# Strassen's scheme for the input product of two FFNs in a float32 transformer forward pass

## The chip, the cores and the metric

The kernel runs on one core of a Trainium2 chip. A core has five engines that run side by side, each with its own queue of instructions: TensorE (PE in the profile; its weight loads are listed apart as PEld), VectorE (DVE), ScalarE (ACT), GpSimd (POOL) and SyncE (SP), which here issues the transfers from the chip's memory (HBM) to the on-chip memory (SBUF). TensorE writes its sums to PSUM, from which VectorE and ScalarE read. The metric is the device time of one execution in microseconds. Three runs of the kernel before gave 1662.89, 1662.97 and 1663.38 us: median 1662.97.

## The reference

Two layers work on 256 latent tokens (LAT) and 256 context tokens (CTX) of width 1024, all in float32. Layer 0 is half FFN, attention, half FFN; layer 1 is half FFN, mLSTM, half FFN, and the last one is computed for the latent tokens alone. So there are four half FFNs; the change is in the second (layer 0, after attention) and the third (layer 1, before mLSTM):

```python
def half_ffn(h, shift, scale, gate, w_in, w_out, g, b):
    xm = modulate(h, shift, scale)               # h * (1 + scale) + shift
    a, u = jnp.split(xm @ w_in, 2, axis=-1)      # w_in: 1024 x 5632
    y = (jax.nn.silu(a) * u) @ w_out             # w_out: 2816 x 1024
    return post_norm(h, 0.5 * gate * y, g, b)    # LayerNorm(ALPHA * h + ...)
```

`shift`, `scale` and `gate` are slices of `silu(c) @ ada_w + ada_b`, nine per layer and one set for each of the two conditioning vectors (latent, context). Since they don't depend on the tokens, the kernel computes them ahead, in pieces, on VectorE: these pieces are the "dots" below.

## The kernel before

Activations lie transposed: 128 partitions carry 128 of the 1024 features, `xh[:, k, :]` holds block k (0 to 7) for 512 columns, of which 0 to 255 are LAT and 256 to 511 are CTX. Every float32 operand x of a large product is split into a rounded part h and the remainder l = x - h (`split`: a cast on ScalarE, then a subtraction on VectorE), and each 128 x 128 block of a product is three matmuls, `mm3`: wh by xh, wh by xl, wl by xh (lines 227, 230, 231 of the profile). Weights come in chunks of 128 x 1024 floats, 512 KB each, over SP's queue into one of three `raw` buffers (RAW = 3), and their split goes to one of seven `w` buffers (WB = 7).

The hidden width 2816 is 22 blocks of 128, called units. `ffn` works in two halves (`hf` = 0, 1) of 11 units. In each half come first the input products: unit j multiplies its block of the columns of `w_in`, for both parts (a and u), with all eight blocks of x, into two PSUM banks; `ffn_g` makes silu(a) * u and splits it. Then come the output products: for each of the eight output blocks d, `unit_out` adds up 11 blocks of `w_out` with the 11 stored units, and VectorE adds the result, times the gate, to h. Units 0 to 3 of a FFN (LEAD = 4) are done for LAT and CTX apart, 256 columns at a time, since the LayerNorm of the FFN or mixer before them ends for LAT first. So are the last four output blocks (TAIL = 4) of the second half. All other input and output products have 512 columns.

A unit takes two chunks of `w_in`, eight blocks each. Before, the blocks of a chunk alternate between a and u: block `k * 2 + part`.

Dots: `ada` loads one chunk of `ada_w` (`ada_load`, two `ada` buffers, the same queue of SP) and multiplies it with the silu of a conditioning row kept in `cb`, 1024 columns, with a running sum (`ada_dot`), once or twice, for one or two conditioning vectors. `side(...)` hands `ffn` a function that is called after each unit and after each output block of the first half, and that issues the next two items of a queue. `queue[1]` (40 items of two vectors, used in the second FFN) and `queue[2]` (32 items of one vector, used in the third) are the ones that the change touches.

The order within an engine's queue is made by a scheduler from the order of the program, priorities and its own estimates of durations; an engine executes its queue strictly in that order, so an instruction that waits holds up those behind it. Buffers of a pool with n copies are reused as they come free, and the wait for that is put in by the framework. PSUM has six `mm` banks for these products and two others.

Of the kernel before, what the change touches and what calls it, by code (L numbers as in the profile page):

```python
# [9 lines left out]
F32 = mybir.dt.float32  # L10
F32R = mybir.dt.float32r
# [3 lines left out]
ALU = mybir.AluOpType  # L15
# [107 lines left out]
C_MASK = 128  # L123
C_ROPE = C_MASK + 2 * TL
C_N = C_ROPE + 4 * P


class Stream:
# [29 lines left out]
class Body:  # L158
# [65 lines left out]
    def mm3(self, out, w, x, first, last, pin=False):  # L224
        (wh, wl), (xh, xl) = w, x
        mm = self.nc.tensor.matmul
        ins = mm(out, wh, xh, start=first, stop=False)  # L227
        if pin:
            self.pin(ins)
        mm(out, wh, xl, start=False, stop=False)  # L230
        mm(out, wl, xh, start=False, stop=last)  # L231

    def x(self, d, g):
        return self.xh[:, d, g[0] : g[1]], self.xl[:, d, g[0] : g[1]]
# [38 lines left out]
    def silu_c(self):  # L273

        pool = ExitStack()
        self.n += 1
        p = pool.enter_context(self.tc.tile_pool(name=f"cp{self.n}", bufs=1, side="right"))
        self.cb = self.t([P, 2, D], pool=p)
        return pool

# [27 lines left out]
    def ada_load(self, layer, dt):  # L308
        if (layer, dt // ND) not in self.mod:
            self.mod[layer, dt // ND] = self.t([P, 2, ND])  # L310
        r = self.t([P, 1024], tag="ada", bufs=2, pool=self.gp)
        self.nc.sync.dma_start(r, self.a["ada_w"][layer, dt])
        return r

# [235 lines left out]
            V.tensor_tensor(out=sl, in0=sl, in1=pu[:, :n], op=ALU.mult)  # L550
        self.split(sl, gh[:, t0:t1], gl[:, t0:t1])

    def ffn(self, layer, s, gate, groups, side, start=None):
        nc, V = self.nc, self.nc.vector
        li = layer * 2 + s
        allg = BOTH
        call = lambda *k: side.get(k, lambda: None)()
        with self.tc.tile_pool(name=f"ffn{li}", bufs=1) as gp:
            self.gp, self.gt, self.gw, self.gn = gp, {}, T, NFH
            done = 0  # L560
            if start:
                start(self)
                done = NSTART

            def unit_in(j, w, g, steps={}, ks=range(ND), ps=None):
                n = g[1] - g[0]
                pa, pu = ps or (self.mm(), self.mm())
                for k in ks:
                    for part, o in ((0, pa), (1, pu)):
                        self.mm3(o[:, :n], w(k * 2 + part), self.x(k, g), k == 0, k == ND - 1)  # L570
                    self.steps(steps.get((j, k), ""))
                if ks[-1] < ND - 1:
                    return pa, pu
                self.ffn_g(j, pa, pu, g)

            def unit_out(hf, d, w, g, steps={}):
                t0, t1 = g
                y = self.mm()
                for i in range(NFH):
                    gh, gl = self.gt[hf * NFH + i]  # L580
                    self.mm3(y[:, : t1 - t0], w(d * NFH + i), (gh[:, t0:t1], gl[:, t0:t1]), i == 0, i == NFH - 1)
                    self.steps(steps.get((int(g == CTX), d - (ND - TAIL), i), ""))
                for gg in groups:
                    if gg[0] >= t0 and gg[1] <= t1:
                        v = 0 if gg[0] == 0 else 1
                        z = self.h[:, d, gg[0] : gg[1]]
                        V.scalar_tensor_tensor(z, y[:, gg[0] - t0 : gg[1] - t0], gate()[:, v, d : d + 1], z, ALU.mult, ALU.add)  # L587
                        if hf:
                            self.add_sum(gg, d)

            w_in, w_out = self.a["ffn_in"][li], self.a["ffn_out"][li]
            stream = lambda j: Stream(self, [w_in[2 * j + i] for i in range(2)])
            for hf in range(2):
                js = list(range(hf * NFH, (hf + 1) * NFH))[0 if hf else done :]
                if hf == 0 and not start:
                    first = js[:LEAD]
                    ws = {j: Keep(self, [w_in[2 * j + i] for i in range(2)], SH) for j in first}
                    assert len(self.running) == 1

                    k0, k1 = range(ND // 2), range(ND // 2, ND)  # L600
                    for j in first[:-1]:
                        unit_in(j, ws[j], LAT, LEADSTEP[li])
                    j = first[-1]
                    ps = unit_in(j, ws[j], LAT, ks=k0)
                    assert not self.running
                    pc = unit_in(first[0], ws[first[0]], CTX, ks=k0)
# [7 lines left out]
                    js = js[LEAD:]  # L614
                for j in js:
# [9 lines left out]
                body = ND - TAIL if hf else ND  # L625
                for d in range(body):
                    unit_out(hf, d, w, allg)
                    call("out", hf, d)
                if body < ND:
                    w = Keep(self, w.chunks, SH, w)  # L630
                    self.fine = True
                    for g in groups:
                        for d in range(body, ND):
                            unit_out(hf, d, w, g, TAILSTEP)
                    self.steps('B')


    def ffn_last(self, layer, gate):
# [3 lines left out]
        with self.tc.tile_pool(name="ffnl", bufs=1) as gp:  # L642
# [9 lines left out]
            def unit_in(j, g, steps={}):  # L652
                n = g[1] - g[0]
                w, pa, pu = stream(j), self.mm(), self.mm()
                for k in range(ND):
                    for part, o in ((0, pa), (1, pu)):
                        self.mm3(o[:, :n], w(k * 2 + part), self.x(k, g), k == 0, k == ND - 1)
                    self.steps(steps.get((j, k), ""))
                return pa, pu

# [798 lines left out]
def emit(ctx, tc, a, out):  # L1459
# [5 lines left out]
    both2 = (0, 1)  # L1465
    queue = [
        [(0, p, both2) for p in range(16, 72)],
        [(1, p, both2) for p in range(40)],
        [(1, p, (0,)) for p in range(40, 72)],
    ]  # L1470
    made = {}

    def once(key, f):
        def get():
            if key not in made:
                made[key] = f()
            return made[key]
        return get

    def side(key, coef, keep=(True, True), nxt=True, ada=(), alone=False):  # L1480
        def pop():
            for _ in range(3 if len(ada) > 40 else 2):
                if ada:
                    b.ada(*ada.pop(0))

        get = once(key, coef)

        b.begin = lambda g: b.norm(g, get, keep[0 if g == LAT else 1], nxt, alone)
        s = {}
        for j in range(NF):  # L1490
            s["in", j] = pop
        for d in range(ND):
            s["out", 0, d] = pop
        return s

    both = (LAT, CTX)
# [4 lines left out]
    cpool = b.silu_c()  # L1501
    b.silu_load()
    b.silu()
    b.ffn(0, 1, once("g1", lambda: b.half_gate(0, 8)), both, side("n2", lambda: b.ln_mod(0, 2, (1, 0)), ada=queue[1]))
    assert not queue[1]
    b.ffn(1, 0, once("g2", lambda: b.half_gate(1, 2)), both, side("n3", lambda: b.ln_mod(1, 0, (1, 3)), (True, False), ada=queue[2]))
    assert not queue[2]
    cpool.close()
# [7 lines left out]
def _layout(inputs):  # L1516
# [13 lines left out]
    w_in = w.reshape(4, NF, P, 2, 1024).transpose(0, 1, 3, 2, 4).reshape(4, 2 * NF, P, 1024).copy()  # L1530
    A["ffn_in"] = w_in
# [73 lines left out]
```

## Time and profile before

| what | value |
|---|---|
| median of the runs | 1662.97 us |
| profiled execution: span | 1662.0 us (1.0 below the median of the runs; instructions from first to last) |
| TensorE busy | 1639.8 us, 99% |
| TensorE weight loads | 1439.4 us, 87% |
| VectorE busy | 1209.0 us, 73% |
| ScalarE busy | 670.5 us, 40% |
| second FFN, units of 512 columns begin | 610.78 us |
| third FFN, units of 512 columns begin | 978.38 us |

A group's row gives the line in the kernel, the engine, the operation, what it writes and reads (all tiles are called t), the shape, the count, then total busy time, the mean in ns, and the idle time of the engine before such an instruction with what ended it. A row of the timeline gives start, length, engine, line, operation, and in brackets the idle time ahead of it and what ended that. Matmuls are pipelined: one's printed length reaches into the next, so what one costs is the distance from start to start.

### The profile page before, as it was taken

To read this page: it belongs to the slowest core of one execution; us is meant where nothing else is said; L and a number is where in the kernel's file an instruction comes from. 1 tells how busy PE (TensorE), PEld (TensorE's weight loads), DVE (VectorE), ACT (ScalarE), POOL (GpSimd) and SP (SyncE) were. 2 spreads that over 40 slices of the span, in tenths; PEclk is the share of its full clock that TensorE was granted. 3 is DMA by queue.
4 is the path that set the end of the run, shared out by engine and by line. 5 is a ranking of instruction groups with operands and counts; after the bars stand their busy time and mean duration, and the time that the engine had idled before them with its cause. 6 is when DMAs were issued, how large, how long until landed. Compare 5 with 4: busy or idle time off the path is not lost. (4 is left out here: it accounts for less than half of the span.)

```text
span 1662.0 us, 24616 instructions
## 1 busy us (share of the span) xinstructions
PE 1639.8 (99%) x9516; PEld 1439.4 (87%) x9516; DVE 1209.0 (73%) x2465; ACT 670.5 (40%) x1117; POOL 62.3 (4%) x76
## 2 busy tenths in 40 slices
PE   9999999999989999999999999999999999999998
PEld 6888888899978998888888998888889989999987
DVE  5899977749888989995334967643335967897687
ACT  5532132214766443312321433322321666656542
POOL 0000000001010200000000100000000100020000
PEclk9999999999999999999999999999999999999999
DMA  9577755412103246674231257642221332337552
GB/s 372 190 230 238 241 203 200 142 64 83 64 1 129 89 166 219 224 251 148 95 101 65 102 191 243 213 152 101 89 101 58 113 128 77 129 113 254 175 181 89
DMA packets 71909, 250.36 MB, mean 151 GB/s; under 512 B 7920, under 2 KB 10736, under 8 KB 71792
## 3 DMA queue, kind: packets, MB, share of 16 engines
q1 hardware_dynamic: 71216, 248.00, 43.8%
q8 instruction: 74, 1.21, 0.3%
q10 hardware_dynamic: 576, 0.79, 0.1%
q14 instruction: 43, 0.35, 0.1%
HBM read 247.71 MB, written 1.05 MB: 150 GB/s over the span
## 5 line engine op out<-in xcount | busy, mean ns | idle before, releaser
L227 PE MATMUL t<-t,t 128*128 128x512 f32 (+2 forms) x2540 | 855.9, 338 | 4.1 <-ACT t L210 3.1
L230 PE MATMUL t<-t,t 128*128 128x512 f32 (+2 forms) x2540 | 857.1, 338 | 2.2 <-DVE t L215 1.2
L231 PE MATMUL t<-t,t 128*128 128x512 f32 (+2 forms) x2540 | 854.1, 337 | 0.1
L215 DVE TENSOR_TENSOR t<-t,t 128x256 fp32r<-128x256 f32 (+3 forms) x680 | 462.1, 716 | 197.2 <-ACT t L210 196.1
L210 ACT CAST t<-t 128x1024 fp32r<-128x1024 f32 (+3 forms) x461 | 381.1, 852 | 547.9 <-PE t L231 301.0
L227 PEld LDWEIGHTS t<-t,t 128*128 128x128 f32 x2540 | 478.0, 189 | 57.6 <-ACT t L210 4.7
L230 PEld LDWEIGHTS t<-t,t 128*128 128x128 f32 x2540 | 478.0, 188 | 56.2 <-DVE t L503 1.8
L231 PEld LDWEIGHTS t<-t,t 128*128 128x128 f32 x2540 | 477.9, 188 | 52.3 <-DVE t L215 0.7
L318 DVE SCALAR_TENSOR_TENSOR t<-t,t 128x1024 bf16<-128x1024 f32 x224 | 262.8, 1222 | 12.2 <-DMA t<-in_ada_w 11.7
L550 DVE TENSOR_TENSOR t<-t,t 128x512 f32<-128x512 f32 (+1 forms) x93 | 54.2, 585 | 111.0 <-PE t L231 90.8
L549 ACT ACTIVATE t<-t 128x512 f32<-128x512 f32 (+1 forms) x93 | 47.5, 514 | 187.1 <-PE t L231 187.1
L587 DVE SCALAR_TENSOR_TENSOR t<-t,t,t 128x256 f32<-128x256 f32 x96 | 42.7, 479 | 52.4 <-PE t L231 52.4
L788 PE MATMUL t<-t,t 128*128 128x256 f32 (+1 forms) x256 | 79.5, 310 | 0.0
L790 PE MATMUL t<-t,t 128*128 128x256 f32 (+1 forms) x256 | 78.8, 308 | 0.0
L789 PE MATMUL t<-t,t 128*128 128x256 f32 (+1 forms) x256 | 78.4, 306 | 0.0
L445 POOL TENSOR_TENSOR t<-t,t 128x256 f32<-128x256 f32 x30 | 23.6, 786 | 1144.2 <-ACT t L435 1142.9
L1303 PE MATMUL t<-t,t 128*128 128x512 f32 (+3 forms) x286 | 60.2, 365 | 2.0 <-ACT t L1380 1.0
L716 PE MATMUL t<-t,t 128*128 128x512 f32 (+1 forms) x300 | 60.5, 364 | 0.0
L1303 PEld LDWEIGHTS t<-t,t 128*128 128x128 f32 (+2 forms) x286 | 43.7, 159 | 18.5 <-issue 2.5
L716 PEld LDWEIGHTS t<-t,t 128*128 128x128 f32 x300 | 51.5, 189 | 8.9
L435 ACT ACTIVATE t<-t 128x256 f32<-128x256 f32 x72 | 26.1, 411 | 66.5 <-DVE t L428 66.5
L789 PEld LDWEIGHTS t<-t,t 128*128 128x128 f32 x256 | 48.3, 189 | 2.5
(189 smaller groups left out, 1062.0 us busy)
## 6 DMA issues: line engine op xcount, KB each, us to landing
t<-in_ffn_in SPq DMA_DIRECT2D x168, 512.0 KB, 3.8
t<-in_ada_w SPq DMA_DIRECT2D x137, 512.0 KB, 4.2
t<-in_ffn_out SPq DMA_DIRECT2D x66, 512.0 KB, 3.7
t<-in_ffn_last SPq DMA_DIRECT2D x22, 512.0 KB, 3.5
t<-in_att_in SPq DMA_DIRECT2D x12, 512.0 KB, 3.5
t<-in_att_out SPq DMA_DIRECT2D x8, 512.0 KB, 3.5
t<-in_ml_qk SPq DMA_DIRECT2D x8, 512.0 KB, 3.4
t<-in_ml_v SPq DMA_DIRECT2D x8, 512.0 KB, 3.5
```

Source lines behind the costliest of these rows:

```text
L210: self.behind(self.nc.scalar.copy(h, x))
L215: self.behind(self.nc.vector.tensor_tensor(out=ls, in0=xs, in1=hs.bitcast(F32), op=ALU.subtract))
L227: ins = mm(out, wh, xh, start=first, stop=False)
L230: mm(out, wh, xl, start=False, stop=False)
L231: mm(out, wl, xh, start=False, stop=last)
L318: ins = nc.vector.scalar_tensor_tensor(self.tmp().bitcast(BF16), r, 1.0, self.cb[:, v, :], ALU.mult, ALU.mult, accum_out=to)
L550: V.tensor_tensor(out=sl, in0=sl, in1=pu[:, :n], op=ALU.mult)
L716: pin(nc.tensor.matmul(o, gs[g], ws[k][w][:, i : i + n], start=k == k0 and g == w == 0, stop=k == k1 - 1 and g == 1,))
L788: mm(o, self.xh[:, k, c], wh, start=k == 0, stop=False)
L789: mm(o, self.xh[:, k, c], wl, start=False, stop=False)
L790: mm(o, self.xl[:, k, c], wh, start=False, stop=k == ND - 1)
L1303: mm = lambda *k, **kw: pin(nc.tensor.matmul(*k, **kw))
```

## The change

In the later eleven units (`hf` = 1) of the second and the third FFN, the input product is done by Strassen's scheme in Winograd's form. The stationary side of a unit is a 2 x 2 matrix of blocks: (a, u) by (features 0 to 511, features 512 to 1023); the moving side is (features 0 to 511, features 512 to 1023) by (LAT, CTX). The usual way is eight products of half size each way; the scheme takes seven, and sums of the operands before and of the results after. One such product is four blocks of 128 features times three matmuls, with 256 columns.

- `fast_sums` makes the sums of the moving side once for each FFN, in two calls after output blocks 4 and 5 of the first half (SUMSAT = 4): three new operands `th`, `tl`, and one that overwrites the lower CTX half of `xh`, `xl`.
- `fast_in` does a unit: it makes four sums of the weights on VectorE (`sums`, one buffer), splits 3.5 chunks of operands instead of two, runs the seven products into three PSUM banks (`x`, `yv`, `z`), copies partial results from PSUM on ScalarE between products that add to the same bank, and combines them on VectorE.
- The memory for `th`, `tl`, `sums` is that of `cb` and the `ada` buffers, which are moved to the pool `cp` and given up before output block 4. So all dots of these two FFNs move into the first half: `DOTS` asks for four dots after each of the 11 units and three after each output block, and no dots stand in the later units. Twelve items of `queue[1]` move to `queue[2]`: each FFN then has 56 dots, the second 28 items of two vectors, the third 12 of two and 32 of one. `cb` is loaded and its SiLU taken a second time for the third FFN.
- The blocks of a `w_in` chunk are put in the order of four of a, then four of u (`part_k`), for all FFNs.
- The descriptor scratch memory of dynamic transfers is made smaller (512), and the framework's check on matmul groups is switched off for the fast units.

```diff
+SUMSAT = 4
+DOTS = (4, 3)
...
+def part_k(part, k):
+    return k // 4 * 8 + part * 4 + k % 4
...
-        r = self.t([P, 1024], tag="ada", bufs=2, pool=self.gp)
+        r = self.t([P, 1024], tag="ada", bufs=2, pool=self.cp)
...
+    def fast_sums(self, i):
...
+        a, b = whole(lo, LAT), whole(lo, CTX)
+        V.tensor_tensor(out=a, in0=a, in1=b, op=ALU.subtract)
+        self.split(a, *at(lo, CTX))
+        c = whole(up, CTX)
+        V.tensor_tensor(out=b, in0=c, in1=b, op=ALU.subtract)
+        self.split(b, *made(1))
+        V.scalar_tensor_tensor(a, a, -1.0, c, ALU.mult, ALU.subtract)
+        self.split(a, *made(0))
+        d = whole(up, LAT)
+        V.scalar_tensor_tensor(d, a, -1.0, d, ALU.mult, ALU.subtract)
+        self.split(d, *made(2))
+
+    def fast_in(self, j, w_in, st):
+        nc, V, S = self.nc, self.nc.vector, self.nc.scalar
+        half = 4 * P
+        r0, r1 = (self.raw(w_in[2 * j + i]) for i in range(2))
+        sums = self.t([P, 4 * half], tag="sums", bufs=1, pool=st)
...
+        ws = [self.pair(sh=SH, n=half)] + [self.pair(sh=SH) for _ in range(3)]
+        self.split(a11, *ws[0])
+        self.split(r1, *ws[1])
+        add(s1, a21, a22)
+        add(s2, s1, a11)
+        self.split(sums[:, : 2 * half], *ws[2])
+        add(s4, s2, a12)
+        add(s3, a11, a21)
+        self.split(sums[:, 2 * half :], *ws[3])
...
+        def product(o, name, x, first, last):
+            for k in range(ND // 2):
+                c = slice(k * P, (k + 1) * P)
+                self.mm3(o, [y[:, c] for y in w[name]], x(k), first and k == 0, last and k == ND // 2 - 1, group=False)
...
+        product(x, "a11", of(0, LAT), True, False)
+        S.copy(a[:, :TL], x)
+        product(y, "a12", of(ND // 2, LAT), True, True)
+        product(v, "s1", of(0, CTX), True, False)
+        S.copy(u[:, TL:], v)
+        product(x, "s2", made(0), False, False)
+        S.copy(a[:, TL:], x)
+        product(z, "a22", made(2), True, True)
+        S.copy(u[:, :TL], z)
+        product(v, "s4", of(ND // 2, CTX), False, True)
+        V.tensor_tensor(out=a, in0=a, in1=yv, op=ALU.add)
+        S.activation(a, a, AF.Silu)
+        product(x, "s3", made(1), False, True)
...
+        V.scalar_tensor_tensor(u2, x[:, None, :].broadcast_to([P, 2, TL]), -1.0, u2, ALU.mult, ALU.subtract)
+        V.tensor_tensor(out=a, in0=a, in1=u, op=ALU.mult)
...
+        self.split(a, gh, gl)
...
+                    if fast:
+                        self.fast_in(j, w_in, st)
+                        continue
...
-        [(1, p, both2) for p in range(40)],
-        [(1, p, (0,)) for p in range(40, 72)],
+        [(1, p, both2) for p in range(28)],
+        [(1, p, both2) for p in range(28, 40)] + [(1, p, (0,)) for p in range(40, 72)],
...
+        def dots(n):
+            while n > 0 and ada:
+                n -= len(ada[0][2])
+                b.ada(*ada.pop(0))
```

More of the change, by code (lines that the diff above doesn't have):

```diff
@@ L222, in behind, with mm3 @@
             self.tc.add_manual_dep(ins.ins, last.ins.name, edge, reason="behind the start")
-    def mm3(self, out, w, x, first, last, pin=False):
+    def mm3(self, out, w, x, first, last, pin=False, group=True):
         (wh, wl), (xh, xl) = w, x
-        mm = self.nc.tensor.matmul
+        mm = lambda *k, **kw: self.nc.tensor.matmul(*k, skip_group_check=not group, **kw)
         ins = mm(out, wh, xh, start=first, stop=False)
@@ L551, in ffn_g, with fast_operands, at, whole @@
         self.split(sl, gh[:, t0:t1], gl[:, t0:t1])
-    def ffn(self, layer, s, gate, groups, side, start=None):
+    def fast_operands(self, st):
+        self.th, self.tl = (self.t([P, 3, ND // 2, TL], F32R, pool=st) for _ in range(2))
+    def fast_sums(self, i):
+        V = self.nc.vector
+        lo, up = slice(2 * i, 2 * i + 2), slice(ND // 2 + 2 * i, ND // 2 + 2 * i + 2)
+        made = lambda k: (self.th[:, k, lo, :], self.tl[:, k, lo, :])
+        def at(ks, g):
+            return self.xh[:, ks, g[0] : g[1]], self.xl[:, ks, g[0] : g[1]]
+        def whole(ks, g):
+            o = self.tmp().rearrange("p (k f) -> p k f", k=2)
+            h, l = at(ks, g)
+            V.tensor_tensor(out=o, in0=h.bitcast(F32), in1=l.bitcast(F32), op=ALU.add)
+            return o
+        a, b = whole(lo, LAT), whole(lo, CTX)
[9 more added lines that the diff above has]
+        self.split(d, *made(2))
@@ L554, in ffn @@
+    def ffn(self, layer, s, gate, groups, side, start=None, cpool=None):
         nc, V = self.nc, self.nc.vector
@@ L614, in ffn @@
                     js = js[LEAD:]
+                fast = cpool is not None and hf == 1
                 for j in js:
+                    if fast:
+                        self.fast_in(j, w_in, st)
+                        continue
                     unit_in(j, stream(j), allg)
@@ L625, in ffn @@
                 body = ND - TAIL if hf else ND
+                if fast:
+                    more.close()
                 for d in range(body):
+                    if cpool and not hf and d == SUMSAT:
+                        cpool.close()
+                        self.n += 1
+                        more = ExitStack()
+                        st = more.enter_context(self.tc.tile_pool(name=f"st{self.n}", bufs=1, side="right"))
+                        self.fast_operands(st)
                     unit_out(hf, d, w, allg)
+                    if cpool and not hf and d >= SUMSAT and d - SUMSAT < 2:
+                        self.fast_sums(d - SUMSAT)
                     call("out", hf, d)
@@ L1478, in once, with side @@
         return get
-    def side(key, coef, keep=(True, True), nxt=True, ada=(), alone=False):
+    def side(key, coef, keep=(True, True), nxt=True, ada=(), alone=False, fast=False):
         def pop():
@@ L1490, in side @@
         for j in range(NF):
-            s["in", j] = pop
+            s["in", j] = (lambda: dots(DOTS[0])) if fast else pop
         for d in range(ND):
-            s["out", 0, d] = pop
+            s["out", 0, d] = (lambda: dots(DOTS[1])) if fast else pop
         return s
```

32 lines of the change are left out of this document (24 added, 8 removed).

## The prediction

> **What bounds the kernel now.** I read the page first (busy shares, slices), then the groups with shapes kept apart, then the timeline of TensorE where it is undisturbed, then busy time by stage. Second FFN means layer 0's second half (before: 565 to 930 us), third means layer 1's first (940 to 1310).
>
> ```profile
> span 1662.0 us, 24616 instructions
> PE 1639.8 (99%) x9516; PEld 1439.4 (87%) x9516; DVE 1209.0 (73%) x2465; ACT 670.5 (40%) x1117; POOL 62.3 (4%) x76
> PE   9999999999989999999999999999999999999998
> DVE  5899977749888989995334967643335967897687
> ```
> ```profile
> L227 PE MATMUL t<-t,t 128*128 128x512 f32 x1316 | 513.0, 390 | 0.1
> L230 PE MATMUL t<-t,t 128*128 128x256 f32 x1176 | 331.2, 282 | 1.9 <-DVE t L215 1.2 <-DVE t L503 0.5
> L227 PEld LDWEIGHTS t<-t,t 128*128 128x128 f32 x2540 | 478.0, 189 | 57.6 <-ACT t L210 4.7 <-ACT t L502 1.1 <-ACT t L549 0.5
> ```
> ```profile
> 574.81 0.28 PE L231 MATMUL t<-t,t 128*128 128x256 f32 x1
> ...
> 577.19 0.28 PE L231 MATMUL t<-t,t 128*128 128x256 f32 x1
> 610.78 0.40 PE L227 MATMUL t<-t,t 128*128 128x512 f32 x1
> ...
> 640.04 0.39 PE L227 MATMUL t<-t,t 128*128 128x512 f32 x1
> ...
> 642.08 0.39 PE L227 MATMUL t<-t,t 128*128 128x512 f32 x1
> 899.84 0.28 PE L231 MATMUL t<-t,t 128*128 128x256 f32 x1
> ...
> 908.67 0.28 PE L231 MATMUL t<-t,t 128*128 128x256 f32 x1
> 978.38 0.40 PE L227 MATMUL t<-t,t 128*128 128x512 f32 x1
> ```
> ```profile
> 640.00:687.00 47.00, 47.00 (x209) 38.91 (x209) 46.87 (x83) 18.58 (x30) 0.00 (x0) 1.00 0.65 219
> 760.00:866.00 106.00, 106.00 (x469) 87.82 (x468) 40.78 (x52) 30.09 (x37) 0.00 (x0) 1.00 0.30 101
> 982.00:1018.00 36.00, 36.00 (x160) 29.82 (x159) 27.59 (x45) 12.32 (x17) 0.00 (x0) 1.00 0.80 264
> ```
> TensorE is never idle for long (99%; in the windows, whose first columns are length, PE, PEld, DVE and ACT, it is busy throughout). A matmul's printed length overlaps the next one's, so its price is the distance between starts. Nine 512-wide ones start in 642.08 - 640.04 = 2.04 us: 0.2267 each. The 256-wide ones come in two steady paces: 21 in 2.38 us (574.81 to 577.19), 0.1133 each, and 75 in 8.83 us (899.84 to 908.67), 0.1177 each; a run keeps its pace for dozens of matmuls. VectorE is the second engine: 46.87 of 47 us in the second FFN's first half, 40.78 of 106 in its later eleven units.
>
> **The change, part by part.** *Matmuls.* A later unit has 16 x 3 = 48 matmuls of 512 columns, 48 x 0.2267 = 10.88 us. It gets 7 x 4 x 3 = 84 of 256: 9.89 us at 0.1177, 9.52 at 0.1133. That is 0.99 to 1.36 us a unit, 21.8 to 29.9 for 22. For the second FFN I take the slower pace (the run at 899.84 also follows 512-wide matmuls without a stall): 11 x 0.99 = 10.9. In the third the units follow a stall (below), after which rows show either pace; the middle gives 11 x 1.17 = 12.9. Together 23.8.
>
> *VectorE in a fast unit.*
> ```profile
> L318 DVE SCALAR_TENSOR_TENSOR t<-t,t 128x1024 bf16<-128x1024 f32 x224 | 262.8, 1222 | 12.2 <-DMA t<-in_ada_w 11.7
> L215 DVE TENSOR_TENSOR t<-t,t 128x1024 fp32r<-128x1024 f32 x214 | 260.5, 1223 | 142.4 <-ACT t L210 142.0
> L215 DVE TENSOR_TENSOR t<-t,t 128x256 fp32r<-128x256 f32 x350 | 134.3, 427 | 49.8 <-ACT t L210 49.7
> L210 ACT CAST t<-t 128x1024 fp32r<-128x1024 f32 x287 | 300.4, 1051 | 483.1 <-PE t L231 294.0 <-issue 143.3 <-DMA t<-in_ffn_out 14.5
> L210 ACT CAST t<-t 128x512 fp32r<-128x512 f32 x107 | 64.3, 611 | 43.4 <-DVE t L550 19.2 <-PE t L903 10.5 <-PE t L231 4.9
> 637.91 0.68 DVE L550 TENSOR_TENSOR t<-t,t 128x512 f32<-128x512 f32 x1
> 638.51 1.82 DVE L215 TENSOR_TENSOR t<-t,t 128x1024 fp32r<-128x1024 f32 x2
> 641.41 1.22 DVE L318 SCALAR_TENSOR_TENSOR t<-t,t 128x1024 bf16<-128x1024 f32 x1
> 642.56 1.23 DVE L318 SCALAR_TENSOR_TENSOR t<-t,t 128x1024 bf16<-128x1024 f32 x1
> 644.85 0.88 DVE L524 SCALAR_TENSOR_TENSOR t<-t,t,t 128x256 f32<-128x256 f32 x2
> 645.64 0.68 DVE L550 TENSOR_TENSOR t<-t,t 128x512 f32<-128x512 f32 x1
> 653.35 0.69 DVE L550 TENSOR_TENSOR t<-t,t 128x512 f32<-128x512 f32 x1
> 689.51 0.68 DVE L550 TENSOR_TENSOR t<-t,t 128x512 f32<-128x512 f32 x1
> ```
> Start to start, 1024 columns cost 1.15 us (641.41 to 642.56), 512 cost 0.60 (637.91 to 638.51), and a 512 of the scalar-tensor-tensor kind about 0.67 (an estimate: 0.40 for 256, from the pair at 644.85, plus half of 1.15 - 0.60). A fast unit has three 1024 subtractions, four additions, four other 512 operations and one scalar-tensor-tensor: 3 x 1.15 + 8 x 0.60 + 0.67 = 8.9 us, under 9.5. ScalarE has 3 x 1.05 + 2 x 0.61 for casts, about 0.6 for the SiLU and four PSUM copies of about 0.4: 6.6. In the built order the weights of a unit are made about a unit and a half ahead, and each PSUM copy has two products (2.8 us) before TensorE returns to that bank. So VectorE is at 90% and TensorE stays the bound; the cover ends when waits inside VectorE's queue exceed 0.6 to 1.0 us a unit.
>
> *The sums* (16 additions or subtractions at 0.60 or 0.67, 8 splits): 20 x 0.60 + 4 x 0.67 = 14.7 us of VectorE per FFN, in the eight output blocks of the first half, which take TensorE 8 x 33 x 0.2267 = 59.8 us. In the second FFN these run from 686.9 (610.78 + 7 x 10.88) to 746.7. The order up to 689.51, the last unit's product, is as before. After it VectorE has 16 dots (18.4), the block results (6.4), five splits of output weights (5.8), the sums (14.7) and the weights of the first fast unit (three splits of 1024, five operations of 512: 6.5): 51.8 of the 57 us, and these weights stand ahead of the seventh block's result, some 5 us before they are wanted. Cost: nothing; without that cover, what is late is the third product, microsecond for microsecond.
>
> *The dots moved forward* are where I see a cost, in the third FFN. Of its 56 dots, 32 need one load of 512 KB each (one vector), not one for two, and there are two buffers.
> ```profile
> 982.43 1.48 SPq L312 DMA_DIRECT2D t<-in_ada_w  x2
> 988.25 1.56 SPq L312 DMA_DIRECT2D t<-in_ada_w  x2
> ...
> 1005.86 1.47 SPq L312 DMA_DIRECT2D t<-in_ada_w  x2
> 1012.54 1.57 SPq L312 DMA_DIRECT2D t<-in_ada_w  x2
> 1018.06 1.76 SPq L312 DMA_DIRECT2D t<-in_ada_w  x2
> 985.17 1.22 DVE L215 TENSOR_TENSOR t<-t,t 128x1024 fp32r<-128x1024 f32 x1 [1.62 <-ACT t L210]
> 986.99 1.23 DVE L318 SCALAR_TENSOR_TENSOR t<-t,t 128x1024 bf16<-128x1024 f32 x1 [0.59 <-DMA t<-in_ada_w]
> ```
> A load issued at 982.43 let its dot start at 986.99: 4.56 us, plus 1.15 for the dot that frees the buffer, so 5.7 us for a pair. Six pairs took 1018.06 - 982.43 = 35.6 us, 5.9 each, between 5.5 (1012.54 to 1018.06) and 6.7 (1005.86 to 1012.54). Before, two such dots stood in a unit of 10.88 us, and the rest ran beside the later units; now there are four, 11.4 us, more than the unit. I take 5.7: the other work between pairs (about 3.1 us) fits into the 3.4 us in which VectorE waits.
>
> The stage begins at 978.38, 367.6 after the second FFN's. Its first dots are of two vectors and four a unit, as in the second FFN before, so units 4 to 6 are multiplied at 637.91, 645.64 and 653.35 plus 367.6: 1005.5, 1013.2, 1020.9. The next four come every 11.4 (two pairs), the first some 1 us later for its load: unit 10 at 1067.5, its split about 1069. TensorE reaches its need at 978.38 + 7 x 10.88 + 35 x 0.2267 = 1062.5: a stall of about 6 us. Sixteen single dots are left, eight pairs, to about 1113 (the first pairs partly wait for block results). Behind them in VectorE's queue stand the sums (14.7), four late results (1.6), four additions (2.4), one split (1.15) and small waits: the third kind of weights is ready near 1133.5. TensorE, at the first fast unit from 1120.4, can do three of its seven products and then four more, 5.6 us: it ends at 1139.1 instead of 978.38 + 76.2 + 59.8 + 9.8 = 1124.2. That is 15 us for both stalls. SP's queue had held the next unit's second load behind these loads, and three raw buffers let it catch up only in two or three units: 2 us more. Sum 17; at 5.5 us a pair 14, at 5.9 it is 20, at 6.7 it is 33.
>
> *Small edits.* The new order of the input blocks puts the first u block into the third quarter instead of the first: at each of three FFN starts with quarter splits between nothing (weights are early) and 2 x 0.43 us; I take 0.3 in all. The second load and SiLU of the conditioning rows (two ScalarE operations of 1024) lies beside the 15 us that ScalarE is idle in the windows; if not covered, 2.1 us. The smaller scratch area and the switched-off group check add no instruction: 0.
>
> *Sum:* 23.8 - 17 - 0.3 = 6.5 off the span of 1662.0: 1655.5. The profiled execution stands 1.0 below the median of 1662.97, so 1656.5.
>
> **Rivals.** (A) *The loads hide*: each pair is back in under 5.4 us, or blocks wait for less. For it: VectorE had 8.4 us idle in 982 to 1018. Against: it idled for these loads and for casts. No stall: 1662.97 - 23.8 = 1639, at the faster pace 1633.
> (B) *The load chain eats the gain*, the case on the other side: place, the single-vector dots of the third FFN; price, 16 pairs times what a pair takes above 5.7; it decides from 17 + 16d = 23.8, a pair of 6.1 us. At the largest pair, 6.7, the sum is -9: 1672. For it: the mean of 5.9 is near that point, and VectorE's queue holds casts' waits between (1.62 at 985.17).
> (C) *VectorE becomes the bound in the fast units*: a wait of 0.6 us at each of four casts makes 8.9 + 2.4 = 11.3 us, 0.4 over the old unit: +9 and the 17, 1689. For it: splits wait 142 us in 214 instances. Against: those are stages in which VectorE runs ahead; when it lags, the casts are done.
> (D) *Half-size matmuls are bound by their weights*: 84 loads of 0.189 us, one after another, are 15.9 us a unit, +110: 1773. Against it: the runs at 0.1133 and 0.1177 load weights for every matmul. [...]
>
> **How the numbers follow.** My forecast has 0.55 (1648 to 1662: both paces, a pair of 5.5 to 5.9), A 0.15, B 0.17, C 0.11, D 0.02. A change within 0.2% (1659.6 to 1666.3) is about what a measurement of this kernel can't tell from none. Faster: A and 0.48 of the forecast, 0.63. Same: 0.07 of the forecast, 0.06 of B, 0.01 of C: 0.14. Slower: 0.23. The range takes in most of A and B and leaves out C, D and A's fast end: 1637 to 1672.
>
> **What would show it.** Right: 256-wide matmuls at 0.113 to 0.118 in 22 units of 9.5 to 9.9 us; no gap of TensorE at the second FFN's first fast unit; in the third, a gap near the first output block and one in the first fast unit, with VectorE waiting for ada_w before. Wrong: gaps in every fast unit (C), no gap in the third FFN (A), a pair above 6.1 us (B), starts 0.15 us or more apart (D).

## The result and the profile after

The changed kernel takes 1659.67 us (median of 10 runs, 1655.76 to 1661.94), the kernel before, run beside it, 1663.18 (10 runs, 1661.40 to 1666.49). The ratio is 0.9974, with a 95% interval of 0.9965 to 0.9983: some 4 us faster, where 6.5 were predicted (1656.5). The profiled execution has a span of 1659.1 us, 2.9 under that of before. It took 1661.01 us, 1.3 more than the median, so what its trace shows as lost is somewhat more than the median run loses.

The page of the changed kernel: span, busy times, the slices of TensorE and of the granted clock (tenths; 9 is 90% or more), and one of its groups.

```profile
span 1659.1 us, 26570 instructions
PE 1624.8 (98%) x10308; PEld 1463.5 (88%) x10308; DVE 1354.8 (82%) x2689; ACT 743.6 (45%) x1267; POOL 62.3 (4%) x76
PE   9999999999989999999999999899999999999998
PEclk9999999999999999999999999898999999999999
...
L327 DVE SCALAR_TENSOR_TENSOR t<-t,t 128x1024 bf16<-128x1024 f32 x224 | 263.8, 1221 | 28.2 <-DMA t<-in_ada_w 27.3
```

The last row is the group of the dots, which had 12.2 us of idle time ahead of them before. TensorE is busy for 15 us less, but the span shrank by 2.9 only: it stands idle in slice 26, and the clock shows two dips that the kernel before doesn't have there. Next come busy times by stage: first the second FFN's later eleven units, then the third FFN from its first unit of 512 columns to its last output block of the first half, then its later eleven units. The columns are length; PE, PEld, DVE, ACT and POOL busy, with counts; the granted clock; DMA share and GB/s.

```profile
746.78:855.28 108.50, 108.50 (x925) 108.50 (x924) 95.86 (x125) 65.84 (x108) 0.00 (x0) 1.00 0.39 118
967.19:1114.61 147.42, 139.22 (x603) 114.73 (x602) 120.80 (x207) 38.97 (x57) 0.00 (x0) 0.97 0.70 223
1114.61:1231.78 117.17, 113.00 (x925) 112.01 (x924) 107.43 (x146) 70.60 (x114) 0.00 (x0) 0.96 0.36 116
```

Before, eleven units took 11 x 10.88 = 119.7 us and the 600 matmuls of 512 columns in the middle row 136.0 (600 x 0.2267). So the second FFN gains 119.7 - 108.5 = 11.2. The third loses 147.4 - 136.0 = 11.4 in its first half and gains 119.7 - 117.2 = 2.5 in its second, which should also have been 11.2: its loss is 11.4 + 8.7 = 20.1, its balance +8.9. Both FFNs together give -2.3; the remaining -0.6 lies elsewhere.

Where the 20.1 us are, TensorE's timeline shows (all three matmuls of a block now stand under L234):

```profile
1044.74 6.73 PE L234 MATMUL t<-t,t 128*128 128x512 f32 x29
1059.67 4.63 PE L234 MATMUL t<-t,t 128*128 128x512 f32 x10 [8.20 <-ACT t L218]
...
1119.85 0.39 PE L234 MATMUL t<-t,t 128*128 128x256 f32 x1 [1.55 <-ACT t L218]
1120.58 1.44 PE L234 MATMUL t<-t,t 128*128 128x256 f32 x5 [0.35 <-DVE t L223]
1124.25 7.97 PE L234 MATMUL t<-t,t 128*128 128x256 f32 x39 [2.23 <-ACT t L218]
```

The first gap is in the first output block, where unit 10 is wanted; the others are in the first fast unit, within and behind its first three products (36 matmuls). The splits that end them (cast L218, subtraction L223) wait behind the dots. VectorE's timeline in the same stage, where L559 multiplies one unit's a and u, L327 is a dot, and L578 is the first operation of the sums, and from SP's queue the issue of two loads of `ada_w` (rows between are left out):

```profile
1022.43 0.68 DVE L559 TENSOR_TENSOR t<-t,t 128x512 f32<-128x512 f32 x1
1023.03 1.82 DVE L223 TENSOR_TENSOR t<-t,t 128x1024 fp32r<-128x1024 f32 x2
1024.76 1.22 DVE L327 SCALAR_TENSOR_TENSOR t<-t,t 128x1024 bf16<-128x1024 f32 x1
1026.40 1.23 DVE L327 SCALAR_TENSOR_TENSOR t<-t,t 128x1024 bf16<-128x1024 f32 x1 [0.41 <-DMA t<-in_ada_w]
...
1030.95 1.23 DVE L327 SCALAR_TENSOR_TENSOR t<-t,t 128x1024 bf16<-128x1024 f32 x1 [2.19 <-DMA t<-in_ada_w]
1032.38 1.23 DVE L327 SCALAR_TENSOR_TENSOR t<-t,t 128x1024 bf16<-128x1024 f32 x1 [0.19 <-DMA t<-in_ada_w]
1034.32 0.68 DVE L559 TENSOR_TENSOR t<-t,t 128x512 f32<-128x512 f32 x1
...
1038.29 1.23 DVE L327 SCALAR_TENSOR_TENSOR t<-t,t 128x1024 bf16<-128x1024 f32 x1 [0.41 <-DMA t<-in_ada_w]
...
1058.29 0.68 DVE L559 TENSOR_TENSOR t<-t,t 128x512 f32<-128x512 f32 x1
...
1105.21 1.89 DVE L578 TENSOR_TENSOR t<-t,t 128x512 f32<-128x512 f32 x3
```
```profile
1026.02 1.97 SPq L321 DMA_DIRECT2D t<-in_ada_w  x2
```

Between two units stand four dots, two pairs of loads. From 1022.43 to 1058.29 there are six pairs: 35.86 / 6 = 5.98 us a pair. A unit takes 11.95 us of VectorE's queue while TensorE needs 10.88 for one. In a cycle three of the four dots wait for their load; the one at 1024.76 doesn't: it stood behind two subtractions (1023.03) and started as soon as they ended. The second dot of a pair, on the other buffer, waits every time (1026.40, 1032.38, 1038.29, and so on to 1056.35, 5.99 us apart on average). So the round of that buffer sets the pace: the dot takes 1.15 us, 0.11 later the next load is issued (1027.66, the second of the row of SP), and 4.72 later the next dot starts (1032.38), together 5.98.

One thing wasn't foreseen: the two dips of the clock. Here they are in windows of 3.41 us, first those around the gap in the output block, then those of the first fast unit:

```profile
1052.23:1055.64 3.41, 0.00 (x0) 0.00 (x0) 1.55 (x3) 0.00 (x0) 0.00 (x0) 1.00 0.91 335
1055.64:1059.05 3.41, 0.00 (x0) 0.00 (x0) 2.70 (x6) 0.95 (x3) 0.00 (x0) 0.50 0.77 243
1059.05:1062.47 3.42, 2.80 (x7) 2.22 (x8) 3.22 (x5) 0.57 (x1) 0.00 (x0) 0.50 0.69 214
1062.47:1065.88 3.41, 3.41 (x10) 2.64 (x9) 1.60 (x4) 0.21 (x1) 0.00 (x0) 0.50 0.88 293
1065.88:1069.29 3.41, 3.41 (x17) 2.80 (x16) 2.54 (x4) 0.83 (x1) 0.00 (x0) 1.00 0.41 118
...
1117.09:1120.50 3.41, 1.59 (x12) 1.20 (x10) 3.41 (x8) 1.19 (x3) 0.00 (x0) 1.00 0.00 0
1120.50:1123.91 3.41, 1.44 (x5) 1.14 (x5) 3.41 (x9) 1.13 (x2) 0.00 (x0) 0.50 0.00 0
1123.91:1127.33 3.42, 3.04 (x12) 2.75 (x13) 3.12 (x5) 2.37 (x4) 0.00 (x0) 0.50 0.82 301
1127.33:1130.74 3.41, 3.41 (x18) 3.41 (x17) 2.29 (x3) 1.37 (x4) 0.00 (x0) 0.50 0.02 8
1130.74:1134.15 3.41, 3.41 (x31) 3.41 (x30) 2.17 (x3) 1.40 (x2) 0.00 (x0) 1.00 0.00 0
```

After a window in which TensorE was idle for all or half of the time (0.00 and 1.59 busy) the clock is 0.50 (the column before the last two) for three windows, 10.24 us, and it is back after the first window that TensorE filled. In a half-clock window that is full there are 18 half-size matmuls, in the next one 31. The working stretches at half clock are 1059.67 to 1065.88 and about as much behind 1120.50, so that TensorE does some 3 us of work less in each (an estimate: half of 6.2 us).

### The profile page after: what moved, and what is told of

Its sections match the earlier page's. It is cut to its first block, busy times and chain, and to the rows that moved or that the text cites. A ratio compares the mean times of both kernels' runs of the same rounds, so it can differ in the third digit from the quotient of the medians.

```text
span 1659.1 us, 26570 instructions
## 1 busy us (share of the span) xinstructions
PE 1624.8 (98%) x10308; PEld 1463.5 (88%) x10308; DVE 1354.8 (82%) x2689; ACT 743.6 (45%) x1267; POOL 62.3 (4%) x76
## 5 line engine op out<-in xcount | busy, mean ns | idle before, releaser
L234 PE MATMUL t<-t,t 128*128 128x256 f32 (+2 forms) x8412 | 1332.6, 320 | 19.3 <-ACT t L218 15.1
L234 PEld LDWEIGHTS t<-t,t 128*128 128x128 f32 x8412 | 1199.4, 189 | 140.1 <-ACT t L218 17.6
L218 ACT CAST t<-t 128x1024 fp32r<-128x1024 f32 (+3 forms) x521 | 428.4, 843 | 481.7 <-PE t L234 233.4
L223 DVE TENSOR_TENSOR t<-t,t 128x256 fp32r<-128x256 f32 (+2 forms) x740 | 513.6, 728 | 116.9 <-ACT t L218 113.2
L327 DVE SCALAR_TENSOR_TENSOR t<-t,t 128x1024 bf16<-128x1024 f32 x224 | 263.8, 1221 | 28.2 <-DMA t<-in_ada_w 27.3
L558 ACT ACTIVATE t<-t 128x512 f32<-128x512 f32 (+1 forms) x71 | 34.3, 488 | 95.4 <-PE t L234 95.3
L559 DVE TENSOR_TENSOR t<-t,t 128x512 f32<-128x512 f32 (+1 forms) x71 | 38.9, 552 | 34.4 <-PE t L234 28.0
L822 PEld LDWEIGHTS t<-t,t 128*128 128x128 f32 x300 | 51.5, 189 | 8.9
L534 ACT ACTIVATE t<-t,t 128x256 f32<-128x256 f32 x64 | 29.4, 503 | 56.6 <-DVE t L533 56.5
L894 PEld LDWEIGHTS t<-t,t 128*128 128x128 f32 x256 | 48.3, 189 | 2.6
L895 PEld LDWEIGHTS t<-t,t 128*128 128x128 f32 x256 | 48.2, 188 | 2.6
L896 PEld LDWEIGHTS t<-t,t 128*128 128x128 f32 x256 | 48.1, 188 | 2.5
L602 DVE TENSOR_TENSOR t<-t,t 128x512 f32<-128x512 f32 x66 | 45.3, 686 | 0.6
```

The source lines that it names most:

```text
L218: self.behind(self.nc.scalar.copy(h, x))
L223: self.behind(self.nc.vector.tensor_tensor(out=ls, in0=xs, in1=hs.bitcast(F32), op=ALU.subtract))
L234: mm = lambda *k, **kw: self.nc.tensor.matmul(*k, skip_group_check=not group, **kw)
L327: ins = nc.vector.scalar_tensor_tensor(self.tmp().bitcast(BF16), r, 1.0, self.cb[:, v, :], ALU.mult, ALU.mult, accum_out=to)
L602: add = lambda o, x, y: V.tensor_tensor(out=o, in0=x, in1=y, op=ALU.add)
L822: pin(nc.tensor.matmul(o, gs[g], ws[k][w][:, i : i + n], start=k == k0 and g == w == 0, stop=k == k1 - 1 and g == 1,))
```

## Experiments

My theory: each FFN's scheme gives 11.2 us; in the third, the dots of one vector come no faster than two buffers let their loads come, which makes unit 10 late, then the sums and the third kind of weights of the first fast unit. Rivals: VectorE's own work is what is late; SP's queue or the memory can't bring the chunks faster; the half clock makes a loss of its own.

**One FFN at a time.** In the first kernel the call for the third FFN has the old form, in the second that for the second FFN; both keep the new order of the dots' queues.

```diff
-    b.ffn(1, 0, ..., side("n3", ..., ada=queue[2], fast=True), cpool=cpool)
+    b.ffn(1, 0, ..., side("n3", ..., ada=queue[2]))
```

> The scheme in the second FFN alone; the third FFN as in the kernel before. My theory (the second FFN gains 11.2 us without a stall, everything that is lost is lost in the third) expects 11 us less than the kernel before: near 1652, with the third FFN's units as before and no stretch of half clock there. A rival, that the second FFN's scheme also costs something later (reloaded conditioning rows, other order in the attention), expects less than 9 us gained.

> The scheme in the third FFN alone, with its 44 dots moved forward. My theory (11.2 us of matmul time gained, about 14 lost in gaps of TensorE, about 6 in half clock) expects 9 us more than the kernel before: near 1672. The rival, that part of the third FFN's loss comes from the second FFN's change, expects the time of the kernel before, 1663, or less.

Measured: the second FFN alone 1654.75 us against 1663.31 (ratio 0.9944, 0.9928 to 0.9961: 6.5 to 12.0 us faster); the third alone 1670.68 (1.0041, 1.0026 to 1.0056: 4.3 to 9.3 us slower). Each interval holds what my theory said (11 and 9), but the medians, 8.6 and 7.4, fall short of it, and 8.6 taken alone fits the rival of "less than 9". Its windows speak against that rival: the eleven fast units, and the 1260 matmuls of 512 columns of the third FFN, which at 0.2267 are 285.6 us.

```profile
751.26:859.76 108.50, 108.50 (x925) 108.50 (x924) 95.62 (x125) 65.80 (x108) 0.00 (x0) 1.00 0.38 118
971.63:1258.88 287.25, 285.71 (x1261) 236.23 (x1260) 171.35 (x279) 82.21 (x106) 0.00 (x0) 1.00 0.54 175
```

The gain of 11.2 us is whole, and the third FFN is as long as before but for 1.5 us of waiting. The profiled execution, the slowest of the four (1657.88 us), lost its time elsewhere: its units of 512 columns in the second FFN begin at 615.23 (751.26 - 136.03), 4.5 us later than the changed kernel's (746.78 - 136.03 = 610.75), although both kernels have the same program up to there. In the windows of the kernel with the third FFN alone, its two halves:

```profile
976.48:1122.49 146.01, 139.04 (x602) 114.52 (x601) 122.64 (x210) 39.41 (x58) 0.00 (x0) 0.96 0.68 225
1122.49:1236.77 114.28, 110.76 (x926) 110.14 (x924) 105.40 (x143) 70.65 (x115) 0.00 (x0) 0.99 0.36 119
```

That is 10.0 us and 5.8 us over the undisturbed lengths (136.0 and 108.5), 15.8 lost against 11.2 gained. So the traces put the loss in the third FFN, and the second's change is no part of it that they show. Its size varies with the execution: 15.8 here, in the fastest of the four runs, 20.1 in the changed kernel.

**More loads under way.** The `ada` buffers, two in the changed kernel, are made four, then three.

```diff
-        r = self.t([P, 1024], tag="ada", bufs=2, pool=self.cp)
+        r = self.t([P, 1024], tag="ada", bufs=4, pool=self.cp)
```

> Four buffers for the chunks of ada_w instead of two, nothing else. My theory (the dots of one vector wait for their load, because only two loads can be under way) expects no gap of TensorE in the third FFN, no stretch of half clock, and 20 us less than the changed kernel: near 1640. The first rival, that VectorE's own work is what is late, expects the gaps at 1051 and 1118 us to stay at over half of their length: 1650 or more. The second rival, that SP's queue or the memory can't bring the chunks faster, expects the same.

> Three buffers for the chunks of ada_w. If what counts is how many loads are under way, each about 4.6 us and 1.2 for its dot, then three come in 6.0 us, 2.0 each, and the four dots of a unit take 8.0 us of its 10.9: no gap, and the time of four buffers, 1641 to 1643. If four are needed, because the queue of SP also holds the chunks of w_in and w_out between them, a gap of 2 us or more stays near the first output block and the time is 1645 or more.

Four buffers: 1641.54 us (1641.15 to 1642.62), ratio to before 0.9870 (0.9856 to 0.9885). The windows of the second FFN's fast units and of the third FFN's two halves, the group of the dots, and the start of the sums:

```profile
747.11:855.61 108.50, 108.50 (x925) 108.50 (x924) 94.99 (x123) 65.92 (x108) 0.00 (x0) 1.00 0.38 118
966.43:1102.46 136.03, 136.03 (x602) 112.62 (x601) 131.18 (x229) 44.58 (x64) 0.00 (x0) 1.00 0.71 242
1102.46:1210.96 108.50, 108.50 (x925) 108.50 (x924) 97.12 (x127) 66.00 (x108) 0.00 (x0) 1.00 0.38 118
```
```profile
L327 DVE SCALAR_TENSOR_TENSOR t<-t,t 128x1024 bf16<-128x1024 f32 x224 | 260.2, 1220 | 0.0
```
```profile
1077.11 1.89 DVE L578 TENSOR_TENSOR t<-t,t 128x512 f32<-128x512 f32 x3
```

TensorE is busy throughout in all three stretches, at full clock; the dots wait for nothing (28.2 us in the changed kernel, 27.3 of them for ada_w), and the sums begin 110.7 us after the stage (1077.11 - 966.43) instead of 138.0 (1105.21 - 967.19). The span is 1639.4, 19.7 below that of the changed kernel: the 20.1 us of loss. By the medians, four buffers gain 18.1. VectorE's work is the same, the queue of SP too, and the chunks come at 242 GB/s in that stage against 223, so both rivals fall. One thing beside the buffers changed: the scheduler put the splits behind the four dots, where one had stood between the two pairs. That order was not tried by itself; but VectorE's idle time in the stage fell from 26.6 us (147.42 - 120.80) to 4.9 (136.03 - 131.18), and its dots alone had waited 21.2 there.

Three buffers: 1643.35 us (ratio 0.9873, 0.9857 to 0.9890). The time is 0.35 us above the range expected. The first output block has no gap, as expected, but the first fast unit keeps 2.9 us, which was not:

```profile
966.33:1102.36 136.03, 136.03 (x603) 112.62 (x602) 127.94 (x224) 42.57 (x62) 0.00 (x0) 1.00 0.72 238
1102.36:1213.80 111.44, 108.90 (x925) 108.48 (x924) 100.62 (x131) 67.91 (x111) 0.00 (x0) 1.00 0.41 124
```

So three buffers are enough for the units of 10.88 us, but the dots behind them still end later than with four, 114.7 us after the stage begins and not 110.7.

**The half clock.** Matmuls that nobody reads are put into TensorE's queue in the first output block of the third FFN, ahead of the ones that use the last two units, 9 and 10: 13 and then 24 of them; they add work and change no result.

```diff
+                    if (li, hf, d, i) == (2, 0, 0, NFH - 2):
+                        self.fill(13)
```

> Thirteen matmuls of plain float32 whose result nobody reads, some 7 us together, are put into TensorE's queue where it waits 8.6 us in the third FFN's first output block, so that it does not stand idle there. My theory (the idle time makes the clock drop to half for 10.24 us, which costs about 3 us there) expects the half clock from 1055 to 1066 us to be gone, that of 1120 to 1131 to stay, and 2 to 3 us less than the changed kernel, though the block that TensorE waits for comes no earlier. The rival, that the drop of the clock has another cause, expects it to stay and the time to be the same or up to 1 us longer.

> The changed kernel (two buffers) with 24 idle matmuls in the place of 13, 10.8 us at the 0.45 us that one took, so that TensorE has no gap in the third FFN's first output block. Theory one (the end of the third FFN is set by VectorE's chain of dots, and the half clock in the first output block only shifts waiting from one place to another): no half clock near 1055 us, a longer wait at the first fast unit, and the time of the changed kernel, 1658 to 1663. Theory two (the half clock costs time of its own): 3 us less than the changed kernel, 1655 to 1658.

Thirteen: 1661.29 us (ratio 0.9986, 0.9976 to 0.9995), no gain. The first expectation failed in its terms too: thirteen took 5.8 us and not some 7, a gap of 4.63 us was left, and the half clock still came, for 6.83 us. Twenty-four: 1664.16 us (1.0002, 0.9993 to 1.0011), 4.5 us more than the changed kernel, which neither theory expected (1663 at most). Timeline of TensorE around the fill (L565) and at the first fast unit, and the windows of the two halves, in the kernel with twenty-four:

```profile
1048.54 10.61 PE L565 MATMUL t<-t 128*128 128x256 f32 x48
...
1121.28 0.80 PE L234 MATMUL t<-t,t 128*128 128x256 f32 x2 [5.53 <-ACT t L218]
```
```profile
966.23:1112.76 146.53, 146.53 (x651) 121.72 (x649) 120.21 (x208) 38.16 (x57) 0.00 (x0) 1.00 0.71 225
1112.76:1232.20 119.44, 112.79 (x925) 112.00 (x924) 109.47 (x148) 71.56 (x116) 0.00 (x0) 0.96 0.38 116
```

Now the clock is 1.00 through the first half. The first half still costs 10.5 us over 136.0, the second now 10.9 over 108.5 instead of 8.7; the wait in the first fast unit grew to 5.53 us. What TensorE didn't lose to the clock it waited for later. In the changed kernel, too, the waits behind the first stretch of half clock (1.55 + 0.35 + 2.23 us) are longer than the 3 us that it takes. So that stretch most likely costs nothing, but these runs don't show it cleanly: with the fill the scheduler also mixed the sums and the last dots in another order, and why the kernel became slower stays open. Behind the second stretch no such wait comes, and no run was made without it; by the trace it takes some 3 of the 20.1 us.

**The pace of half-size matmuls.** The fast units go at 108.50 / 924 = 0.1174 us a matmul in both FFNs, and not between the paces in the third. What sets it? The weights of the fast units stand 16 floats into their buffers (`SH`); with four buffers I put them at 0 and at 48.

```diff
-        ws = [self.pair(sh=SH, n=half)] + [self.pair(sh=SH) for _ in range(3)]
+        ws = [self.pair(sh=48, n=half)] + [self.pair(sh=48) for _ in range(3)]
```

> Four buffers, and the weights of the fast units at offset 0 of their buffers instead of 16 floats. With four buffers each of the 22 fast units takes 9.86 us, that is 84 matmuls at 0.1174. If the pace of half-size matmuls (0.1133 or 0.1177) hangs on where weights and moving operand lie to one another, the units change to between 9.52 and 9.9 us each: at most 8 us less than with four buffers alone, 1634. If it doesn't, the time stays at 1641.5.

> As the run with offset 0, with an offset of 48 floats: 1634 to 1642 if the pace hangs on the offset, 1641.5 if it doesn't.

At 0: 1644.58 us (ratio 0.9883, 0.9868 to 0.9897), slower than either answer that was expected. At 48: 1638.80 (0.9846, 0.9831 to 0.9860). Windows of the two fast stages, of the kernel with 0 and of that with 48:

```profile
747.53:857.52 109.99, 109.99 (x925) 109.99 (x924) 95.05 (x123) 65.98 (x108) 0.00 (x0) 1.00 0.38 116
1107.12:1217.12 110.00, 110.00 (x926) 110.00 (x925) 96.96 (x127) 65.78 (x108) 0.00 (x0) 1.00 0.39 116
```
```profile
747.03:853.59 106.56, 106.56 (x925) 106.56 (x924) 95.03 (x123) 65.97 (x108) 0.00 (x0) 1.00 0.39 120
1103.20:1209.76 106.56, 106.56 (x925) 106.55 (x924) 97.26 (x127) 66.06 (x108) 0.00 (x0) 1.00 0.40 120
```

110.0, 108.5 and 106.6 us, each in both FFNs, to 0.01: the pace changed with where the operands lay. A stall before didn't change it: in the changed kernel the ten later units of the third FFN, behind the stall, begin at 1133.12 and take 1231.78 - 1133.12 = 98.7 us, 0.1175 a matmul, against 0.1174 where nothing stalled. By which rule, four more kernels were to tell, which move `th` and `tl` by a tile of padding before or behind them.

```diff
         self.th, self.tl = (self.t([P, 3, ND // 2, TL], F32R, pool=st) for _ in range(2))
+        self.t([P, 56], pool=st)
```

> Four buffers, weights at offset 48, and the sums of the moving side (th, tl) placed 16 floats further on. At offset 48 the products that read xh and xl go at 0.1133 to 0.1136, the three that read th and tl at 0.117. If each product's pace hangs on where its weights and its moving operand lie to one another, the three change and the four stay: down to 0.1133 the units take 9.52 us, 3.5 us less for the 22 than the 1638.8 of the run with offset 48; up to 0.120, 2.5 us more. If it doesn't, 1638.8.

> As the run with th and tl 16 floats further on, with 32: the three products' pace between 0.1133 (1635.3) and 0.120 (1641.3) if it hangs on the places, 0.117 (1638.8) if not.

> Four buffers, weights at offset 48 floats, and th, tl moved so that they begin at a multiple of 256 bytes, as xh and xl do (they began 224 bytes past one). Over the 22 fast units of three runs, the pace went with the distance of the weights from the moving operand, modulo 256 bytes: 0: 0.1196, 32: 0.1183, 64: 0.1167, 96: 0.1184, 192: 0.1135, 224: 0.1172. Here it is 192 for all seven products: 0.1135 each, 9.53 us a unit, 3 us less than the 1637.6 that the same kernel gave with th and tl where they were (mean of three): 1634.6. If another cause sets the pace of the three products, 1637.6 and 0.117 for them.

> The same with th and tl begun 160 bytes past a multiple of 256: the distance is 32 for the three products that read them, so 0.1183 for these by the theory of the distance, 0.117 by any other, and the time within 1 us of 1637.6 either way.

The first two, with the padding in front, left `th` and `tl` where they were by the addresses in the built programs, which no trace holds (the pool is laid out from its far end). So they only repeat the kernel with 48, and the traces agree: 1636.57 and 1637.43 us (0.9836, 0.9820 to 0.9852; 0.9840, 0.9825 to 0.9854), the same paces in every product. The other two did move them, and my rule, a pace for each distance between weights and moving operand, fell:

```profile
1103.63:1212.46 108.83, 108.83 (x926) 108.83 (x925) 97.08 (x127) 65.92 (x108) 0.00 (x0) 1.00 0.39 117
```

With the distance 192 for all products they all go at 0.1178, not at 0.1135 (1642.79 us; 0.9870, 0.9854 to 0.9886); in the other the three products come to 0.1182, near the 0.1183 of my rule (1641.53 us; 0.9859, 0.9838 to 0.9880). Both kernels are slower than either answer expected. And in both, products whose own operands had not moved changed pace too: from 0.1133 to 0.1178 in the first, while in the second three of them alternate from unit to unit between 0.1178 and 0.1133 (0.1158 on average). So the place of a product's own operands didn't set its pace alone; what else did, the neighbours' places or the product before, stays open.

The kernel with four buffers and the weights at 48 beats both kernels: 1636.6 to 1638.8 us in its three runs, 1.5 to 1.6% under the kernel before.

## Why the prediction was nearly right

- **Direction and mechanism held.** Gain from matmuls in both FFNs, no stall in the second, in the third a gap near the first output block and one in the first fast unit, with VectorE waiting for ada_w ahead of both. The time is 3.2 us above the forecast and inside its own range (1648 to 1662).
- **Matmuls, second FFN:** 10.9 predicted, 11.2 measured; the slower of the two paces was the right one to take.
- **Matmuls, third FFN:** 12.9 predicted, by a middle between two paces, "after which rows show either pace"; 11.2 measured. The failing idea was that a stall sets the pace. Both stages have the same length when nothing stalls (108.50 with four buffers), and the pace moved with the addresses (106.6 to 110.0 us a stage).
- **The pair:** 5.7 us predicted, 5.98 measured. The prediction was right that the other work between pairs fits into VectorE's waits: the second dot of each pair waits for its load every time. The term that was too small is the load: 4.56 us, taken from one load, against 4.72 here, and the 0.11 us between a dot and the next issue were left out. The mean of 5.9 that the prediction had from six pairs, and set aside, was nearer. The stage starts 11.2 earlier than before, so predicted times are shifted by that: unit 10 was to be multiplied at 1056.3 and was at 1058.29; the dots were to end at 1101.8 and ended at 1105.21.
- **Stalls:** 17 predicted, 20.1 measured. Undisturbed, TensorE begins the last four products of the first fast unit 136.0 + 36 x 0.1174 = 140.3 us into the stage. The prediction had 15 more; the trace has 1124.25 - 967.19 = 157.1, that is 16.8 more. The dots were 3.4 us late, of which 1.5 came back, since the work behind them took 19.0 and not 20.5. The 2 us in which SP's queue was to catch up did not come: behind that start TensorE has only one wait left, under 0.4 us. What came in their place is the half clock, which was in no term: the 888 matmuls that are left take 1231.78 - 1124.25 = 107.5 us and not 104.3 (888 x 0.1174). So the parts 15 + 2 + 0 were 16.8 + 0 + 3.3, and that 17 lies so near to 20.1 is in part luck. The half clock in the first half most likely only moved loss from the second place to the first (11.4 and 8.7 measured, 6 and 11 predicted).
- **VectorE in a fast unit:** 8.9 us predicted; 95.86 / 11 = 8.7 measured. It held no fast unit up once the loads came early.
- **Small edits:** 0.3 predicted; the rest of the span outside the two FFNs came out 0.6 shorter, which is less than executions differ by.
- **Rivals.** A (the loads hide) is wrong for two buffers and right for four: 1641.5 against its 1639. B (the load chain eats the gain) has the right mechanism; its point of decision, 6.1 us a pair, was missed by 0.12, and with the scheme in the third FFN alone that FFN indeed lost. C and D are out: no gaps in the later fast units, and at full clock no product slower than 0.120 us a matmul.

## What to carry to other kernels

When work is moved into a shorter stage, count the loads it needs against the buffers they can be in: with n buffers, n loads come per load time plus use (measured with two: 5.98 us; for other n an estimate from that), and if the stage asks for more, an engine with slack on average (here 120.80 of 147.42 us busy) still makes the bound wait. Here 18 us by the medians, 20 in the profiled execution, of the 22 that the scheme brought were lost to a pair of buffers of 512 KB each, and four instead of two gave them back. Filling the idle time of an engine that waits again later brought nothing here, so look first at the last link of the chain.

## What the runs showed of the hardware

**The clock changed on a grid of 3.41 us.** In the profiled execution of the changed kernel the clock drops at 461.73, 1055.64 and 1120.50 and is back at 465.14, 1065.88 and 1130.74; from each of these six changes to the next it is 1, 173, 3, 16 and 3 windows of 3.41 us, and 154 more to the last drop, at 1656.39. Not every drop had an empty window ahead of it: 1.59 of 3.41 us were busy at 1117.09, and 1.66 in the kernel before (first row below, with the next window at 0.50). But a window with 1.65 in the same execution (second fence's row) had no drop behind it, nor had one with 1.88 in the kernel with the second FFN alone (1003.90 us). And in the kernel with four buffers and the weights at 48, one with 2.29 had half clock behind it (last fence). So the busy time of a window didn't decide alone; what did stays open.

```profile
457.93:461.34 3.41, 1.66 (x12) 1.22 (x10) 2.82 (x10) 1.75 (x5) 0.00 (x0) 1.00 0.01 2
461.34:464.75 3.41, 3.33 (x14) 3.15 (x15) 3.25 (x12) 2.22 (x8) 0.71 (x1) 0.50 0.00 0
```
```profile
495.47:498.89 3.42, 1.65 (x11) 1.34 (x10) 2.79 (x6) 2.28 (x6) 1.57 (x1) 1.00 0.00 0
```
```profile
927.84:931.25 3.41, 2.29 (x20) 2.09 (x19) 3.41 (x10) 0.96 (x4) 1.03 (x2) 1.00 0.24 46
931.25:934.66 3.41, 3.41 (x19) 3.41 (x18) 2.67 (x13) 0.77 (x2) 0.00 (x0) 0.50 0.79 259
```

**The pace of 256-column matmuls changed with placement.** In the second FFN's fast units of the changed kernel, at full clock and without gaps, the products (12 matmuls each) went at 0.1136 to 0.1192 us a matmul. With one placement a stage took the same time in both FFNs to 0.01 us. Five placements gave stages of 106.56, 108.17, 108.50, 108.83 and 110.00 us, so 0.1153 to 0.1190 a matmul, and 6.9 us between the best and the worst for the two stages of a run.
